# Two activation parts in one 512-column pass, with halves of a bank added on evacuation

## The chip, the cores and the metric

The kernel runs on one core of a Trainium2 chip. TensorE multiplies: it holds a block of 128 by 128 numbers (the stationary operand, brought by a weight load) and streams columns of the other operand past it, into PSUM. VectorE (DVE), ScalarE (ACT) and GpSimd (POOL) do the element-wise work, SyncE (SP) issues most of the transfers. The metric is the device time of one execution in microseconds (us); smaller is better.

## The reference, cut to what matters

Four residual layers over 256 tokens of 1024 features, and a final RMSNorm. Layers 0 and 3 mix tokens with Mamba-2, layer 1 with HGRN2, layer 2 with a gated DeltaNet (below: mamba, hgrn, gdn). Each layer then attends to 256 memory tokens and ends with a gated MLP that has a short convolution. Nearly all arithmetic is products of the 256 tokens with weight matrices, in float32:

```python
for i in range(DEPTH):                                   # DEPTH = 4
    x = x + mixer[i % 3](rmsnorm(x, ln_mix[i]), ...)     # in_w, then scan or recurrence, then out_w
    mem_n = rmsnorm(mem, ln_mem[i])
    x = x + memory_cross_attention(rmsnorm(x, ln_xattn[i]), mem_n, wq, wkv, wo)
    x = x + conv_glu_ffn(rmsnorm(x, ln_ffn[i]), up_w, conv_w, conv_b, down_w)

def conv_glu_ffn(h, up_w, conv_w, conv_b, down_w):       # d_ff = 2816
    gate, up = jnp.split(h @ up_w, 2, axis=-1)
    gate = causal_dwconv(gate, conv_w) + conv_b          # width 3
    return (jax.nn.silu(gate) * up) @ down_w
```

## The kernel before, in words

Features lie on the 128 partitions, tokens along the free dimension. Every product with a weight matrix is made of *steps*: one block of 128 by 128 weights times 256 tokens. To keep float32 accuracy each operand is split into a high and a low part of a format that TensorE takes in one pass (`wH`, `wL` for weights, `hH`, `hL` for activations), and `mm3` (line 164) adds up three products per step: high by high, low by high, high by low. Each of the three is a matmul of 256 columns with its own weight load.

Weights come in *pieces* of 128 by 1024 (8 steps). `prep` (line 150) issues a piece's transfer from SP into `raw`, rounds it to `wH` on ACT (line 158) and subtracts to get `wL` on DVE (line 159). There are 4 buffers of `raw` and 3 each of `wH` and `wL`; `prep` is moved some 300 instructions ahead of its place in the program, so weights are made while TensorE works on earlier ones.

`proj` (line 227) multiplies two pieces into the two halves of one PSUM bank of 512 columns. `ps_acc` (line 105) has four such banks, which rotate; the other four PSUM banks serve the mixers' short products. `out_proj` (line 252) keeps four banks open at once, one for each 256 output features. `mem_kv` (line 342) makes keys and values of the memory tokens; for the values the activations are the stationary operand and 256 weight columns stream.

What reads the bank: in the MLP `gate` (line 460) multiplies it by the token's norm on DVE (line 462) and convolves (lines 300 and 302); in mamba and gdn `conv` (line 295) reads the bank directly, once on ACT and three times on DVE; z is read by a Silu on ACT; keys are scaled on DVE (line 347).

The order of each engine's instructions is fixed when the program is built. A scheduler places instructions by a priority, program order with some groups moved ahead; TensorE's own order is that of the program, in which `Weave` (line 49) puts the mixers' short products among the long ones by a clock of charges (`tick(654)` for two steps). Each engine works its list strictly in order, so an instruction that waits holds up all behind it.

## Time and profile before

| | |
|---|---|
| median of 3 runs | 2111.76 us (2109.93 to 2115.88) |
| span of the profiled execution | 2112.4 us |
| TensorE busy | 2073.2 us, 98% |
| VectorE busy | 1590.7 us, 75% |
| ScalarE busy | 1282.7 us, 61% |
| GpSimd busy | 341.9 us, 16% |

The profiled execution's own time is its span, 2112.4 us, from the first to the last instruction; no time around it is listed apart, and it lies 0.6 us above the median of the runs. "Busy" is the time in which at least one instruction was under way; a matmul's row shows its whole way through the array, 0.28 us, though the next starts 0.12 us later, so rows of matmuls overlap and a busy TensorE is not one at its peak. What a stage can lose or win is read from stretches of the span, stage by stage.

### The profile page before, as it was taken

The numbers are of one execution on the slowest core, as the hardware profiler recorded it, in microseconds if no ns is written. First come the engines' busy times: TensorE is split into PE (matmuls) and PEld (weight loads), VectorE is DVE, ScalarE is ACT, GpSimd is POOL, SyncE is SP. The second block draws the span as 40 slices with busy tenths as digits, with TensorE's granted clock in tenths as the row PEclk, the third lists the DMA queues.
The fourth block names the chain that finished last, engine by engine and source line by source line (L and its number), as shares of the span: only waits on it lengthen the run. The fifth ranks groups of instructions, "written<-read, shape, count | busy, mean of one in ns | idle before, by whom it ended". The sixth has DMA issues, their size and how long they took to land.

```text
span 2112.4 us, 42162 instructions
## 1 busy us (share of the span) xinstructions
PE 2073.2 (98%) x17084; PEld 2022.5 (96%) x17084; DVE 1590.7 (75%) x2423; ACT 1282.7 (61%) x1874; POOL 341.9 (16%) x468
## 2 busy tenths in 40 slices
PE   8999999999999999999998999999999999999998
PEld 8999999999999899999998889999999999999997
DVE  6899787875689778866786775778756999777765
ACT  6677666554565566554676875666545777666553
POOL 2032211000133110001054450110001223101001
PEclk9999999999999999999999999999999999999999
DMA  6544545665644446655543333456555444545563
GB/s 237 165 152 151 157 146 163 204 189 170 195 159 138 141 132 197 193 185 183 183 127 124 112 127 102 136 164 202 188 170 186 156 150 151 163 138 176 185 188 111
DMA packets 110372, 343.10 MB, mean 162 GB/s; under 512 B 15456, under 2 KB 25312, under 8 KB 110176
## 3 DMA queue, kind: packets, MB, share of 16 engines
q1 hardware_dynamic: 106176, 333.42, 49.9%
q10 hardware_dynamic: 3744, 6.71, 1.0%
q8 instruction: 134, 2.20, 0.4%
q0 software_dynamic: 256, 0.26, 0.1%
q14 instruction: 62, 0.51, 0.1%
HBM read 336.42 MB, written 3.93 MB: 161 GB/s over the span
## 4 chain that ended last, share of the span: by engine, by line
PE 82%; issue 5%; DVE 5%; ACT 3%; POOL 2%; DMA 2%; SPq 0%; DVEq 0%; POOLq 0%; ACTq 0%
PE ffps L166 8%; PE ffps L168 8%; PE ffps L167 8%; PE acc L166 7%; PE acc L167 7%; PE acc L168 7%; PE mps L166 4%; PE mps L168 3%; PE mps L167 3%; PE kvps L167 2%; PE kvps L166 2%; PE kvps L168 2%; DVE wL L159 2%; PE qps L168 2%; PE qps L167 2%
## 5 line engine op out<-in xcount | busy, mean ns | idle before, releaser
L159 DVE TENSOR_TENSOR wL<-raw,wH 128x1024 fp32r<-128x1024 f32 (+2 forms) x639 | 775.2, 1214 | 348.5 <-ACT wH L158 347.0
L158 ACT CAST wH<-raw 128x1024 fp32r<-128x1024 f32 (+2 forms) x639 | 657.0, 1029 | 562.5 <-PE ffps L167 170.6
L166 PE MATMUL acc<-aH,wH 128*128 128x256 f32 x1408 | 402.3, 287 | 0.6 <-ACT aH L171 0.6
L168 PE MATMUL acc<-aH,wL 128*128 128x256 f32 x1408 | 399.2, 284 | 0.1
L167 PE MATMUL acc<-aL,wH 128*128 128x256 f32 x1408 | 398.6, 283 | 0.1
L166 PE MATMUL ffps<-hH,wH 128*128 128x256 f32 x1408 | 396.1, 282 | 1.8 <-ACT hH L181 1.8
L167 PE MATMUL ffps<-hL,wH 128*128 128x256 f32 x1408 | 396.0, 281 | 0.0
L168 PE MATMUL ffps<-hH,wL 128*128 128x256 f32 x1408 | 395.7, 281 | 0.0
L166 PEld LDWEIGHTS acc<-aH,wH 128*128 128x128 f32 x1408 | 269.1, 192 | 3.4 <-issue 1.3
L167 PEld LDWEIGHTS acc<-aL,wH 128*128 128x128 f32 x1408 | 269.9, 192 | 1.5 <-issue 0.5
L168 PEld LDWEIGHTS acc<-aH,wL 128*128 128x128 f32 x1408 | 269.9, 192 | 0.5 <-DVE wL L159 0.3
L166 PEld LDWEIGHTS ffps<-hH,wH 128*128 128x128 f32 x1408 | 265.0, 188 | 2.7 <-ACT hH L181 2.6
L168 PEld LDWEIGHTS ffps<-hH,wL 128*128 128x128 f32 x1408 | 265.3, 188 | 0.7 <-DVE wL L159 0.7
L167 PEld LDWEIGHTS ffps<-hL,wH 128*128 128x128 f32 x1408 | 265.3, 188 | 0.5
L166 PE MATMUL mps<-hH,wH 128*128 128x256 f32 x768 | 220.5, 287 | 0.0
L168 PE MATMUL mps<-hH,wL 128*128 128x256 f32 x768 | 215.9, 281 | 0.0
L167 PE MATMUL mps<-hL,wH 128*128 128x256 f32 x768 | 215.7, 281 | 0.0
L201 POOL TENSOR_TENSOR ns<-nsq 128x256 f32<-128x256 f32 x13 | 10.7, 827 | 880.4 <-ACT nsq L198 880.4
L166 PEld LDWEIGHTS mps<-hH,wH 128*128 128x128 f32 x768 | 144.7, 188 | 2.7 <-issue 2.4
L167 PEld LDWEIGHTS mps<-hL,wH 128*128 128x128 f32 x768 | 144.7, 188 | 0.3
L168 PEld LDWEIGHTS mps<-hH,wL 128*128 128x128 f32 x768 | 144.6, 188 | 0.1
L168 PE MATMUL gps<-hH,wL 128*128 128x256 f32 x448 | 128.0, 286 | 0.3 <-DVE wL L159 0.3
(397 smaller groups left out, 4514.5 us busy)
## 6 DMA issues: line engine op xcount, KB each, us to landing
raw<-f_up SPq DMA_DIRECT2D x176, 512.0 KB, 3.5
raw<-m_in SPq DMA_DIRECT2D x96, 512.0 KB, 3.5
raw<-f_down SPq DMA_DIRECT2D x80, 512.0 KB, 3.5
raw<-xa_kv SPq DMA_DIRECT2D x60, 512.0 KB, 3.8
raw<-g_in SPq DMA_DIRECT2D x48, 512.0 KB, 3.8
raw<-m_out SPq DMA_DIRECT2D x32, 512.0 KB, 3.5
raw<-xa_q SPq DMA_DIRECT2D x32, 512.0 KB, 3.6
raw<-xa_o SPq DMA_DIRECT2D x32, 512.0 KB, 3.5
```

The costliest lines, as they stand in the source:

```text
L158: ACT.copy(H[:, c], raw[:, c])
L159: DVE.tensor_tensor(out=L[:, c], in0=raw[:, c], in1=f32(H[:, c]), op=ALU.subtract)
L166: PE.matmul(dst, aH, bH, start=start, stop=False, skip_group_check=True)
L167: PE.matmul(dst, aH, bL, start=False, stop=False, skip_group_check=True)
L168: PE.matmul(dst, aL, bH, start=False, stop=stop, skip_group_check=True)
L201: self.eng.tensor_tensor(out=self.sum, in0=sq[:, :T], in1=sq[:, T:], op=ALU.add)
```

## The change

The high and low parts of the activations now lie side by side in one tile (`hh`), and one matmul of 512 columns passes both by the high weights (`mm2`); a second one of 256 columns adds high activations by low weights. A step has two matmuls instead of three. Its result fills a whole bank, whose two halves are added when it is read (`fold`: a copy of one half on ACT, an addition on DVE). So a product of two pieces takes two banks, and `ps_acc` has two buffers of two banks instead of four of one. `out_proj` of mixers and attention and hgrn's `proj_tok` keep `mm3`; the MLP's down product becomes `down_proj`, which makes the output in two halves. Values stream 512 weight columns, from two pieces made by `prep2` in a pool of their own. Convolutions and Silus read the folded copy in SBUF; the MLP's multiplication by the norm is on POOL for the first 20 of 22 tiles, and the split of its result is done as tiles come instead of in the down product. The charges of `tick` are adapted.

```diff
-    ps_acc = ctx.enter_context(tc.tile_pool(name="ps_acc", bufs=4, space=PSUM))
+    ps_acc = ctx.enter_context(tc.tile_pool(name="ps_acc", bufs=2, space=PSUM))
...
+    def banks(name):
+        return ps_acc.tile([P, 2, 512], F32, tag="acc", name=name)
     def bank(name):
-        return ps_acc.tile([P, 512], F32, tag="acc", name=name)
+        return banks(name)[:, 0, :]
...
-    hH = cst.tile([P, KT, T], F32R, name="hH")
-    hL = cst.tile([P, KT, T], F32R, name="hL")
+    hh = cst.tile([P, KT, 2, T], F32R, name="hh")
+    hH, hL = hh[:, :, 0, :], hh[:, :, 1, :]
...
+    def prep2(srcs, pool):
+        with tc.high_priority(offset=PRIO):
+            raw = pool.tile([P, 2, 1024], F32, tag="raw2", name="raw2")
+            H = pool.tile([P, 2, 1024], F32R, tag="wH2", name="wH2")
+            L = pool.tile([P, 2, 1024], F32R, tag="wL2", name="wL2")
+            for i in range(2):
+                nc.sync.dma_start(out=raw[:, i, :], in_=srcs[i])
+                ACT.copy(H[:, i, :], raw[:, i, :])
+                DVE.tensor_tensor(out=L[:, i, :], in0=raw[:, i, :], in1=f32(H[:, i, :]), op=ALU.subtract)
+        return H, L
...
+    def mm2(dst, wH, wL, both, start, stop):
+        PE.matmul(dst, wH, both, start=start, stop=False, skip_group_check=True)
+        PE.matmul(dst[:, :T], wL, both[:, 0, :], start=False, stop=stop, skip_group_check=True)
+    def fold(ps, dst, n=2):
+        ACT.copy(dst, ps[:, :n, T:])
+        return DVE.tensor_tensor(out=dst, in0=ps[:, :n, :T], in1=dst, op=ALU.add)
+    def proj(srcs, ps, both=None):
+        both = hh if both is None else both
         for i, s in enumerate(srcs):
             H, L = prep(s)
             for kt in range(KT):
                 c = slice(kt * P, (kt + 1) * P)
-                mm3(ps[:, i * T:(i + 1) * T], H[:, c], L[:, c], hH[:, kt, :], hL[:, kt, :],
-                    i == 0 and kt == 0, kt == KT - 1)
+                mm2(ps[:, i, :], H[:, c], L[:, c], both[:, kt], kt == 0, kt == KT - 1)
                 if kt % 2:
-                    weave.tick(654)
+                    weave.tick(616)
...
+    def down_proj(wsrc, nk, aa, last):
+        st = Stats(DVE if last else POOL)
+        ng = (nk + 3) // 4
+        for half in range(2):
+            accs = [banks(f"acc{j}") for j in range(2)]
+            for g in range(ng):
+                n = min(4, nk - 4 * g)
+                for j in range(2):
+                    H, L = prep(wsrc[g, 2 * half + j], n * T)
+                    for cb in range(2):
+                        for k in range(n):
+                            kt = 4 * g + k
+                            c = slice(k * T + cb * P, k * T + (cb + 1) * P)
+                            mm2(accs[j][:, cb, :], H[:, c], L[:, c], aa[:, kt], kt == 0, kt == nk - 1)
...
+        for b in range(4):
+            ps = banks("kvps")
...
+            fold(ps, KTt[:, 2 * b:2 * b + 2, :])
...
+        with phase(f"vw{layer}", 2) as vw:
+            for b in range(2):
+                ps = banks("vps")
+                for kh in range(2):
+                    H, L = prep2([io["xa_kv"][layer, 1, 2 * b + i, kh] for i in range(2)], vw)
+                    for mt in range(2):
+                        for k in range(4):
...
+                            mm3(ps[:, mt, :], mm[:, kt, 0, t], mm[:, kt, 1, t], H[:, :, c], L[:, :, c], kt == 0, kt == KT - 1)
...
-            def gate(t, ps):
-                gu = wk.tile([P, 2, T], F32, tag="gu", name="gu")
-                DVE.tensor_tensor(out=gu, in0=ps.rearrange("p (a b) -> p a b", a=2),
-                                  in1=rs.unsqueeze(1).to_broadcast([P, 2, T]), op=ALU.mult)
+            def gate(t, gu):
+                (DVE if t > 19 else POOL).tensor_tensor(out=gu, in0=gu, in1=rs.unsqueeze(1).to_broadcast([P, 2, T]), op=ALU.mult)
...
+                if t % 2:
+                    split(a2[-1], aa[:, t - 1:t + 1, 0, :], aa[:, t - 1:t + 1, 1, :])
...
+                ps = banks("ffps")
                 proj([io["f_up"][layer, 2 * t + i] for i in range(2)], ps)
-                todo.append((t, ps))
+                gu = wk.tile([P, 2, T], F32, tag="gu", name="gu", bufs=3)
+                fold(ps, gu)
+                todo.append((t, gu))
...
+                        src = np_.tile([P, 2, T], F32, tag="tmp", name="src", bufs=3)
+                        fold(ps, src)
                         for i in range(2):
                             ti = [16 + g, 24 + g, 2 * g, 2 * g + 1][2 * u + i]
-                            conv(cc[:, 2 * u + i, :], ps[:, i * T:(i + 1) * T], lambda j: pcol("m_cw", (ia * 32 + ti) * 4 + j),
+                            conv(cc[:, 2 * u + i, :], src[:, i, :], lambda j: pcol("m_cw", (ia * 32 + ti) * 4 + j),
```

Three places show what moves. The first is TensorE at the start of the first MLP's up product; `ffps` is the bank. Before:

```order
2544 L166 MATMUL ffps<-hH,wH 128x256
2545 L167 MATMUL ffps<-hL,wH 128x256
2546 L168 MATMUL ffps<-hH,wL 128x256
2547 L166 MATMUL ffps<-hH,wH 128x256
2548 L167 MATMUL ffps<-hL,wH 128x256
2549 L168 MATMUL ffps<-hH,wL 128x256
```

And of the change:

```order
1913 L245 MATMUL ffps<-hh,wH 128x512
1914 L246 MATMUL ffps<-hh,wL 128x256
1915 L245 MATMUL ffps<-hh,wH 128x512
1916 L246 MATMUL ffps<-hh,wL 128x256
1917 L245 MATMUL ffps<-hh,wH 128x512
1918 L246 MATMUL ffps<-hh,wL 128x256
```

The same 768 columns per step pass in two matmuls instead of three.

The second is VectorE while the keys of layer 2 are made. `KTt<-kvps` reads a bank of keys, `nh` and `hL` (after: `hh`) normalize the tokens for the mixer, and the `wL` of 384 columns is the first weight of the mixer. Before:

```order
955 L159 TENSOR_TENSOR wL<-raw,wH 128x1024
956 L171 TENSOR_TENSOR hL<-nh,hH 128x256 x2
957 L221 SCALAR_TENSOR_TENSOR nh<-xT,prm,nrs 128x256 x2
958 L347 TENSOR_TENSOR KTt<-kvps,rsm 128x512
959 L159 TENSOR_TENSOR wL<-raw,wH 128x1024
960 L171 TENSOR_TENSOR hL<-nh,hH 128x256 x2
961 L221 SCALAR_TENSOR_TENSOR nh<-xT,prm,nrs 128x256 x2
962 L159 TENSOR_TENSOR wL<-raw,wH 128x1024
963 L171 TENSOR_TENSOR hL<-nh,hH 128x256 x2
964 L347 TENSOR_TENSOR KTt<-kvps,rsm 128x512
965 L159 TENSOR_TENSOR wL<-raw,wH 128x1024 x6
966 L159 TENSOR_TENSOR wL<-raw,wH 128x384
```

And of the change, where row 997 folds the second bank pair of keys and row 999 the third:

```order
988 L163 TENSOR_TENSOR wL<-raw,wH 128x384
989 L237 SCALAR_TENSOR_TENSOR nh<-xT,prm,nrs 128x256
990 L187 TENSOR_TENSOR hh<-nh,hh 128x256
991 L237 SCALAR_TENSOR_TENSOR nh<-xT,prm,nrs 128x256
992 L187 TENSOR_TENSOR hh<-nh,hh 128x256
993 L237 SCALAR_TENSOR_TENSOR nh<-xT,prm,nrs 128x256
994 L187 TENSOR_TENSOR hh<-nh,hh 128x256
995 L237 SCALAR_TENSOR_TENSOR nh<-xT,prm,nrs 128x256
996 L187 TENSOR_TENSOR hh<-nh,hh 128x256
997 L251 TENSOR_TENSOR KTt<-kvps,KTt 128x512
998 L187 TENSOR_TENSOR hh<-nh,hh 128x256
999 L251 TENSOR_TENSOR KTt<-kvps,KTt 128x512
```

The reading of a bank of keys has moved behind the mixer's first weight and eight instructions of the normalization.

The third is VectorE in the first MLP, where the memory tokens of the next layer are split (`mL<-mtmp`, after: `mm<-mtmp`). Before:

```order
440 L462 TENSOR_TENSOR gu<-ffps,nrs 128x512
441 L159 TENSOR_TENSOR wL<-raw,wH 128x1024
442 L182 SCALAR_TENSOR_TENSOR mL<-mtmp,prm,mH 128x256 x3
443 L159 TENSOR_TENSOR wL<-raw,wH 128x1024
444 L182 SCALAR_TENSOR_TENSOR mL<-mtmp,prm,mH 128x256 x3
445 L462 TENSOR_TENSOR gu<-ffps,nrs 128x512
446 L159 TENSOR_TENSOR wL<-raw,wH 128x1024
```

And of the change:

```order
440 L163 TENSOR_TENSOR wL<-raw,wH 128x1024
441 L529 TENSOR_TENSOR a_4153<-c,gu 128x256
442 L163 TENSOR_TENSOR wL<-raw,wH 128x1024
443 L198 SCALAR_TENSOR_TENSOR mm<-mtmp,prm,mm 128x256 x3
444 L163 TENSOR_TENSOR wL<-raw,wH 128x1024
445 L198 SCALAR_TENSOR_TENSOR mm<-mtmp,prm,mm 128x256 x3
446 L251 TENSOR_TENSOR gu<-ffps,gu 128x512 x2
```

Two folds now stand together behind two weight pieces and six splits of memory tokens.

## Rows read from the trace of the kernel before

**Rows 1.** Page, part 1: busy us, share, instructions of each engine.
```profile
PE 2073.2 (98%) x17084; PEld 2022.5 (96%) x17084; DVE 1590.7 (75%) x2423; ACT 1282.7 (61%) x1874; POOL 341.9 (16%) x468
```

**Rows 2.** Waits of TensorE: total us, times, longest; the two longest rows.
```profile
PE kvps L166 <- ACT wH L158: 6.6, 1, 6.6
PE grp L1033 <- ACT S L1028: 4.8, 2, 3.0
```

**Rows 3.** Stretches: mamba (layer 0), MLP up, MLP down, hgrn, gdn.
```profile
core 0: us, PE busy (x) PEld busy (x) DVE busy (x) ACT busy (x) POOL busy (x), PEclk, DMA share, GB/s
60.00:226.00 166.00, 165.33 (x1362) 157.60 (x1360) 154.39 (x272) 120.99 (x170) 40.11 (x34) 1.00 0.48 153
...
338.00:464.00 126.00, 125.56 (x1055) 125.03 (x1055) 100.49 (x145) 72.35 (x104) 3.35 (x5) 1.00 0.61 192
464.00:527.00 63.00, 63.00 (x528) 63.00 (x527) 33.79 (x37) 30.14 (x36) 1.18 (x2) 1.00 0.56 171
...
574.00:686.00 112.00, 111.96 (x946) 105.34 (x945) 98.80 (x148) 65.92 (x90) 36.22 (x18) 1.00 0.47 150
...
1021.00:1250.00 229.00, 217.70 (x1739) 205.23 (x1738) 181.21 (x358) 173.64 (x259) 96.08 (x218) 0.99 0.41 131
```

**Rows 4.** TensorE in order of time, split products: start us, duration us.
```profile
1000.07 0.28 PE L166 MATMUL kvps<-wH,mH 128*128 128x256 f32 x1
1000.19 0.28 PE L167 MATMUL kvps<-wL,mH 128*128 128x256 f32 x1
```

**Rows 5.** TensorE in order of time, plain float32 products of gdn.
```profile
1070.28 1.03 PE L911 MATMUL gp<-kq 128*128 128x256 f32 x4
1071.14 0.27 PE L949 MATMUL gkp<-ident,kq 128*128 128x128 f32 x1
```

**Rows 6.** Groups by line and shape, MLP up: xcount, busy us, mean ns, idle before.
```profile
L166 PE MATMUL ffps<-hH,wH 128*128 128x256 f32 x1408 | 396.1, 282 | 1.8 <-ACT hH L181 1.8
```

**Rows 7.** Groups by line and shape, VectorE, ScalarE and GpSimd.
```profile
L159 DVE TENSOR_TENSOR wL<-raw,wH 128x1024 fp32r<-128x1024 f32 x612 | 757.5, 1239 | 323.9 <-ACT wH L158 322.5
L158 ACT CAST wH<-raw 128x1024 fp32r<-128x1024 f32 x612 | 641.3, 1048 | 528.9 <-PE ffps L167 170.6 <-PE acc L167 140.6 <-PE kvps L168 42.0
...
L204 POOL TENSOR_TENSOR ns<-ns,nsq 128x256 f32<-128x256 f32 x78 | 76.7, 983 | 47.4 <-ACT nsq L198 43.2
...
L462 DVE TENSOR_TENSOR gu<-ffps,nrs 128x512 f32<-128x512 f32 x88 | 60.3, 689 | 19.3 <-PE ffps L168 18.9
...
L302 DVE SCALAR_TENSOR_TENSOR cc<-mps,prm,cc 128x255 f32<-128x255 f32 x64 | 30.5, 476 | 0.1
...
L171 ACT CAST pH<-pt 128x512 fp32r<-128x512 f32 x16 | 9.4, 590 | 4.7 <-PE pt L418 4.7
```

**Rows 8.** VectorE in order of time, in mamba of layer 0.
```profile
123.32 1.21 DVE L159 TENSOR_TENSOR wL<-raw,wH 128x1024 fp32r<-128x1024 f32 x1
124.45 0.48 DVE L554 TENSOR_SCALAR E<-rb,tcol 128x256 f32<-128x256 f32 x1
...
125.49 0.68 DVE L171 TENSOR_TENSOR aL<-yT,aH 128x512 fp32r<-128x512 f32 x1
126.09 0.68 DVE L594 TENSOR_TENSOR yT<-yT,sz 128x512 f32<-128x512 f32 x1
```

**Rows 9.** A line of VectorE: duration ns min/median/max, first and last start.
```profile
L182 DVE SCALAR_TENSOR_TENSOR hL<-xT,prm,hH x64: 471/478/972, 270.4 to 1914.1; 128x256 fp32r<-128x256 f32 x64
```

**Rows 10.** A line of VectorE in mamba, the same columns.
```profile
L605 DVE SCALAR_TENSOR_TENSOR yT<-yT,prm,rs x32: 471/798/1243, 114.4 to 1835.3; 128x256 f32<-128x256 f32 x32
```

**Rows 11.** Groups by line and shape, VectorE in the normalization.
```profile
L221 DVE SCALAR_TENSOR_TENSOR nh<-xT,prm,nrs 128x256 f32<-128x256 f32 x32 | 14.1, 479 | 0.6 <-ACT nrs L213 0.5
...
L171 DVE TENSOR_TENSOR hL<-nh,hH 128x256 fp32r<-128x256 f32 x32 | 12.4, 420 | 0.6 <-ACT hH L171 0.2
```

**Rows 12.** Stretches of 3 us at the start of the queries of layer 1.
```profile
721.00:724.00 3.00, 2.13 (x13) 1.53 (x13) 3.00 (x5) 1.43 (x3) 1.31 (x3) 0.97 0.27 109
724.00:727.00 3.00, 3.00 (x16) 3.00 (x16) 0.93 (x2) 1.04 (x1) 1.41 (x2) 0.50 0.58 175
```

More of the change, by code (lines that the diff above doesn't have):

```diff
@@ L250, in proj_tok, with new_x, add, out_proj @@
                         weave.tick(654)
-    def out_proj(wsrc, nk, a, gens=None, gname=None, layer=0, last=False):
-        accs = [bank(f"acc{b}") for b in range(4)]
-        ng = (nk + 3) // 4
-        st = Stats(DVE if last else POOL)
+    def new_x(b, add, st, gname, layer, last):
+        xs = flat(xT[:, 2 * b:2 * b + 2, :])
+        add(xs)
+        if gname is not None:
+            for kt in (2 * b, 2 * b + 1):
+                split_gain(xT[:, kt, :], pcol(gname, layer * 8 + kt), hH[:, kt, :], hL[:, kt, :])
+        st.add(xs)
+        if last:
+            for kt in (2 * b, 2 * b + 1):
+                fg = pcol("final", kt)
+                if b < 3:
+                    POOL.tensor_scalar(out=KTt[:, kt, :], in0=xT[:, kt, :], scalar1=fg, scalar2=None, op0=ALU.mult)
+                else:
+                    ACT.activation(out=KTt[:, kt, :], in_=xT[:, kt, :], func=AF.Copy, scale=fg)
+    def down_proj(wsrc, nk, aa, last):
+        st = Stats(DVE if last else POOL)
+        ng = (nk + 3) // 4
+        for half in range(2):
[9 more added lines that the diff above has]
+                            mm2(accs[j][:, cb, :], H[:, c], L[:, c], aa[:, kt], kt == 0, kt == nk - 1)
+                    if g == ng - 1:
+                        def add(xs, ps=accs[j]):
+                            x3 = xs.rearrange("p (a b) -> p a b", a=2)
+                            for i in range(2):
+                                DVE.tensor_tensor(out=x3, in0=x3, in1=ps[:, :, i * T:(i + 1) * T], op=ALU.add)
+                        new_x(2 * half + j, add, st, None, 0, last)
+        return st
+    def out_proj(wsrc, nk, a, gens=None, gname=None, layer=0):
+        accs = [banks(f"acc{b}") for b in range(2)]
+        accs = [accs[b // 2][:, b % 2, :] for b in range(4)]
+        ng = (nk + 3) // 4
+        st = Stats()
         for g in range(ng):
@@ L384, in attention @@
+                            weave.tick(600)
+                for mt in range(2):
+                    ACT.activation(out=Vt[:, mt, b * 512:(b + 1) * 512], in_=ps[:, mt, :], func=AF.Copy, scale=rsmc[:, mt:mt + 1])
     def attention(layer, st):
@@ L743, in hgrn @@
             for pr in range(4):
-                ps = bank("fps")
+                ps = banks("fps")
                 proj([io["h_in"][ib, pr, i] for i in range(2)], ps)
                 e1 = W("e1", 1)
-                ACT.activation(out=flat(e1), in_=ps, func=AF.Exp, scale=-1.0)
+                fold(ps, e1)
+                ACT.activation(out=e1, in_=e1, func=AF.Exp, scale=-1.0)
                 DVE.tensor_scalar(out=e1, in0=e1, scalar1=1.0, scalar2=None, op0=ALU.add)
@@ L1065, in unit @@
             def unit(piece, tis, cc):
-                ps = bank("gps")
+                ps = banks("gps")
                 proj([io["g_in"][ic, piece + i] for i in range(2)], ps)
-                if tis is not None:
-                    with tc.high_priority(offset=EVAC):
-                        for i in range(2):
-                            conv(cc[:, i, :], ps[:, i * T:(i + 1) * T], lambda j: pcol("g_cw", tis[i] * 4 + j), 4, None)
-                return ps
+                with tc.high_priority(offset=EVAC):
+                    if tis is None:
+                        fold(ps, cc)
+                        return
+                    src = np_.tile([P, 2, T], F32, tag="tmp", name="src", bufs=3)
+                    fold(ps, src)
+                    for i in range(2):
+                        conv(cc[:, i, :], src[:, i, :], lambda j: pcol("g_cw", tis[i] * 4 + j), 4, None)
             gens = []
```

121 lines of the change are left out of this document (50 added, 71 removed).

## The prediction

> **What bounds the kernel now.** I read the page's busy times first: TensorE 2073.2 us of a span of 2112.4 [rows 1]. Overlapping rows make a matmul engine look busy, so I next read who TensorE waited for: the longest entries are 6.6 us, once, at the start, and 4.8 us in two waits [rows 2]. It waits for almost nothing, so TensorE's own list sets the time. Third, the stretches by stage: the reader should compare VectorE with the length of each. It is busy 154.39 of 166 us in mamba, 98.80 of 112 in hgrn, 100.49 of 126 in the MLP's up product, 181.21 of 229 in gdn [rows 3]. So TensorE is the bound everywhere, and in mamba VectorE stands 11.6 us behind it. Last, TensorE in order of time: split matmuls of 256 columns start 0.12 us apart [rows 4]. The clock is granted in full there, the 2.4 GHz level, at which 256 columns would take 106.7 ns. Some 13.3 ns of each interval are not columns.
>
> **What those 13.3 ns are.** In plain float32 the same shape starts 0.86 / 4 = 215 ns apart [rows 5], two clock periods for each of 256 columns (213.3 ns) and only 2 ns more, though each of these matmuls too has its own load of 128 by 128 weights. [...] Where 512 split columns stream, their 213.3 ns hide the next load as rows 5 do: I take 216 ns. The 256 columns that follow hide the next load no better than now: 120 ns. The bounds for 512 columns are 213 (columns alone) and 240 (twice rows 4).
>
> **What is removed.** A step falls from 3 x 120 = 360 to 216 + 120 = 336 ns. Steps that change: MLP up 1408 [rows 6], mamba 768, gdn 384, queries 256, hgrn 192, MLP down 704, keys 256; 3968 in all, counted from the loops (pieces times 8). 3968 x 24 ns = 95.2 us. Values: 256 steps of 3 x 120 ns become 128 of 3 x 216 ns, 92.2 against 82.9, 9.2 us less. Together **104.4 us**, to 2008.0, if nothing else becomes late.
>
> **What is added to ScalarE and VectorE.** A fold is a copy of 512 columns out of PSUM, 590 ns on ScalarE, and an addition of 512 on VectorE, for which the MLP's multiplication is the nearest row, 689 ns [rows 7]; back to back such an operation holds VectorE 0.60 us, a weight piece 1.13 [rows 8]. Products with a fold: 48 in the mambas, 88 in MLPs, 24 in gdn, 16 queries, 12 in hgrn, 16 keys. Keys and the MLP had one reading of that size already.
>
> *Mamba.* VectorE needs 154.4 + 24 x 0.60 = 168.8 us, TensorE now 166 - 384 x 0.024 = 156.8. VectorE becomes the bound: 12 us given back in each of two layers, **24**. Some of its list can slip into the output product behind, and some will wait; I let these cancel. Bounds: 0 and 40.
>
> *MLP up.* 100.5 + 22 x 0.60 for folds + 11 x 0.60 for splits that were in the down product - 20 x 0.60 for multiplications now on POOL = 108.3 us, against 126 - 8.4 = 117.6 on TensorE. This hides, but the POOL work costs VectorE something: a line with two SBUF inputs that reads 478 ns as its median reaches 972 [rows 9], and in mamba another has a median of 798 where its least is 471 [rows 10]; there POOL is busy 40.11 us of 166 [rows 3]. With 0.5 us for each of 20 multiplications VectorE comes to 118.3, just late: 2 us a layer, **8** (0 to 40).
>
> *Keys.* With two buffers, the fourth product of the keys needs the bank pair of the second. Its fold stands in VectorE's list behind the mixer's first weight piece, and that piece's buffer is free only when TensorE is through with the third product (the change's second place in the order). From there: rounding (0.5 to 1.05 us), subtraction (0.5 to 1.13), then normalization at 0.40 and 0.34 us each (durations 479 and 420 less the overlap) [rows 11], then the fold. Layer 1: 1.05 + 1.13 + 3 x 0.40 + 5 x 0.34 + 0.60 = 5.7; layer 2, whose first piece is small (0.5 us each, by proportion), 0.5 + 0.5 + 4 x 0.74 + 0.60 = 4.6; layer 3 about 4.6. In layer 0 the first fold stands behind two weight pieces of that kind, about 5. TensorE stands still: **20**. With four banks it had two products more to go on with.
>
> *Where the memory tokens are split.* In three MLPs two folds stand behind a weight piece that waits for the product before (the third place). ScalarE: 1.05 + 3 x 0.40 + 0.50 for the copy, then 0.60 and some 0.2 of signals: 3.6 us each, **11**. At the start of each mamba the softplus chain and a weight piece stand so before a fold, 1.05 + 1.13 + 0.60 + 0.3 = 3.1 us, **6**.
>
> *gdn.* The tile for z is now claimed before the head two places back has freed it, so its fold waits for that head's end and one of two bank pairs is held meanwhile; the next products run in a single pair and wait for their folds, 1.4 us plus the queue. About four such places at 2 us: **8** (0 to 20). hgrn, 98.8 + 12 x 0.60 = 106 us of VectorE against 107.4, and the two halves of the down product, whose first bank pair must be read before the second half starts: **6** together (2 to 12).
>
> *The clock.* After 3 us in which TensorE was busy 2.13, the granted clock reads 0.50, the 1.2 GHz level, and TensorE shows 16 matmuls in 3 us [rows 12] where 25 fit at 0.12: 1.1 us lost. Eight of the new standstills last 3 us or more: **9**.
>
> The sum: 2112.4 - 104.4 + 24 + 8 + 20 + 11 + 6 + 8 + 6 + 9 = 2100.0. The span is 0.6 us over the median, which I leave. **2100 us**, 0.6% faster. A measurement tells no change from one within 0.3% here, 2105.4 to 2118.1.
>
> **The rivals.**
>
> *The buffers absorb it (faster).* VectorE's backlog in mamba slips into the output product, and gdn's other products cover its folds. For it: TensorE shows 98% although VectorE is at 93% in mamba. Against it: 168.8 is over 156.8 whatever the order. Left are the standstills that the order fixes, 20 + 11 + 6 and 4 for the clock: 2008 + 41 = 2049.
>
> *VectorE loses to POOL (slower).* Every convolution in mamba, which now has two SBUF inputs where the bank was one at 476 ns [rows 7], and every convolution and weight piece of the MLP meets POOL as in rows 9 and 10. A POOL addition of 256 takes 983 ns, so a multiplication of 512 is about 1.7, 34 us in each MLP. It decides once VectorE is past TensorE's 117.6, that is from 0.47 us for each multiplication; at 0.75 it adds 20 x 0.25 x 4 = 20 us, and mamba's convolutions about 4 each: 2128. Against it: weight pieces have a mean of 1239 over all stages, near the 1.21 of one alone [rows 7, 8].
> The Trainium skill ("SBUF — State Buffer", section Who interferes with whom) states that a VectorE instruction with two SBUF inputs and a GpSimd instruction that reads SBUF shut each other out for the whole instruction. By that rule the 34 us would come on top of 108.3 in each MLP, 25 us over TensorE, and the time would be near 2190; the mean of 1239 for weight pieces speaks against so much, and I give it 2 in 100.
>
> *The excess goes with each matmul (slower).* If 512 columns start 226.7 ns apart, a step is 346.7 ns and the saving 3968 x 13.3 ns + 5.1 = 58 us. The losses to VectorE shrink to 76, as TensorE is later: 2130. Against it: rows 5. At 240 ns nothing is saved, 2177.
> The Trainium skill ("TensorE: Matmul & The Clock Gate", section Back-to-back issue gap) gives columns over 2.4 GHz plus 2.5 ns, 109 and 216 ns; the trace's 0.12 us disagrees at 256. By it a step would have been 327.5 and become 325, and the time would be near 2165; 1 in 100.
>
> **How the numbers follow.** My forecast 45 in 100, with 2080 to 2120 as its own range; absorbed 23; VectorE and POOL 18 with the 2 of the rule; the excess 13 with its 1; the rest spread. Faster: three fifths of the forecast (27) and the absorbed (23), 50. Within 0.3%: a quarter of the forecast and a few of each slower rival, 19. Slower: 31. The range leaves out one in ten on either side: 2055, under which only a wholly absorbed case lies, and 2140, above which the rules and the upper bounds lie.
>
> **What would show it.** Starts of `ffps` matmuls 0.216 and 0.120 us apart (0.227 or 0.240: the excess rival). Mamba's stretch as long as now or longer, with VectorE at 95% or more; if it is under 160 us, absorbed is right. In the keys one idle time of TensorE of about 5 us a layer, released by a fold; in three MLPs one of 3 to 4. MLP up near 122 us; 130 or more is POOL's doing. I am wrong altogether if TensorE shows waits under 40 us in sum and the time is still over 2100, or if the down products, where VectorE is busy 33.79 of 63 us [rows 3], do not shorten by about 3 us each.

## The result and the profile after

| | before | after |
|---|---|---|
| median of 4 runs | 2111.73 us (2109.93 to 2115.88) | 2344.23 us (2338.53 to 2347.89) |
| ratio, 95% interval | | 1.109 [1.107, 1.112] |
| span of the profiled run | 2112.4 us | 2336.7 us |

The change made the kernel 11% slower, far outside the range of the prediction. What answers to [rows 1] in the page after:

```profile
PE 2129.8 (91%) x12732; PEld 1835.8 (79%) x12732; DVE 1729.3 (74%) x2551; ACT 1385.6 (59%) x2066; POOL 490.1 (21%) x564
```

TensorE went from 98% to 91%. Its waits (answer to [rows 2]; total us, times, longest) name the reason in the first lines: it waits for folds (L251), for the additions that read down's bank pairs (L314), and in the mambas for a sum on GpSimd (`s`, L664), which is no reader of a product. All its waits add up to 195 us, before to 31 us.

```profile
PE ffps L245 <- DVE gu L251: 30.6, 8, 10.2
PE kvps L245 <- DVE KTt L251: 22.8, 4, 6.9
PE gn L667 <- POOL s L664: 19.2, 10, 4.2
PE acc L245 <- DVE xT L314: 12.2, 4, 3.1
PE gps L245 <- DVE src L251: 11.4, 3, 4.6
PE kvps L245 <- DVE xT L314: 9.1, 3, 3.1
```

The stretches, in the order of [rows 3] (mamba of layer 0, MLP up, MLP down, hgrn, gdn):

```profile
66.00:248.00 182.00, 169.31 (x987) 140.80 (x986) 175.96 (x285) 128.54 (x190) 42.03 (x34) 0.98 0.43 136
368.00:513.00 145.00, 131.40 (x728) 112.18 (x729) 116.47 (x151) 88.08 (x134) 36.72 (x26) 0.96 0.54 167
513.00:583.00 70.00, 65.29 (x355) 56.07 (x354) 35.73 (x42) 30.39 (x35) 2.21 (x3) 0.95 0.53 165
640.00:752.00 112.00, 111.65 (x753) 95.96 (x752) 100.59 (x155) 72.06 (x101) 36.87 (x18) 1.00 0.45 139
1125.00:1388.00 263.00, 230.05 (x1333) 192.87 (x1332) 192.16 (x369) 186.70 (x278) 89.23 (x206) 0.92 0.36 112
```

Mamba is 16 us longer, up 19, down 7, gdn 34; hgrn is the same, though its folds and products changed too. The granted clock (the column behind the engines', 1.00 is the 2.4 GHz level) fell in every stretch that grew.

The second thing to see is the spacing of the products (answer to [rows 4]; TensorE in order of time, start and duration): the up projection, the values, and the up projection behind a stop.

```profile
417.97 0.40 PE L245 MATMUL ffps<-hh,wH 128*128 128x512 f32 x1
418.21 0.28 PE L246 MATMUL ffps<-hh,wL 128*128 128x256 f32 x1
418.33 0.39 PE L245 MATMUL ffps<-hh,wH 128*128 128x512 f32 x1
...
439.39 0.63 PE L245 MATMUL ffps<-hh,wH 128*128 128x512 f32 x1
439.82 0.41 PE L246 MATMUL ffps<-hh,wL 128*128 128x256 f32 x1
440.03 0.63 PE L245 MATMUL ffps<-hh,wH 128*128 128x512 f32 x1
...
1794.76 0.39 PE L182 MATMUL vps<-wH,mm 128*128 128x512 f32 x1
1794.99 0.39 PE L183 MATMUL vps<-wL,mm 128*128 128x512 f32 x1
```

512 columns take 0.24 us, not 0.216 (over all up products at the full clock the median is 232 ns, a quarter at 229 or less, a quarter at 240 or more; the values' 227), and 256 take 0.12. Behind the stop, at the 1.2 GHz level, the same two take 0.43 and 0.21.

A reckoning from the starts of TensorE's list: intervals over 0.7 us add up to 214.6 us (98 of them), before 24.8 us (18), so 190 us more. Products that start while the clock is at its half fill 114.9 us, before 13.4; half of that is extra, 51 us more. 190 + 51 = 241, which is 17 more than the growth of the span, 224.3. In those 17 must lie what the wide products gain; they were not taken apart further.

One of the stops, at the memory tokens of layer 0 (ScalarE, VectorE and TensorE, a fence each, in order of time, with the idle time before and its releaser):

```profile
427.10 1.05 ACT L162 CAST wH<-raw 128x1024 fp32r<-128x1024 f32 x1 [0.51 <-issue]
431.99 0.51 ACT L197 ACTIVATE mm<-mtmp,prm 128x256 fp32r<-128x256 f32 x1 [3.84 <-DMA mtmp<-mem]
...
435.74 0.89 ACT L197 ACTIVATE mm<-mtmp,prm 128x256 fp32r<-128x256 f32 x2
436.54 0.56 ACT L250 COPY gu<-ffps 128x512 f32<-128x512 f32 x1
```

```profile
435.87 1.28 DVE L198 SCALAR_TENSOR_TENSOR mm<-mtmp,prm,mm 128x256 fp32r<-128x256 f32 x3
437.14 1.29 DVE L251 TENSOR_TENSOR gu<-ffps,gu 128x512 f32<-128x512 f32 x2
```

```profile
437.98 0.76 PE L245 MATMUL ffps<-hh,wH 128*128 128x512 f32 x1 [9.91 <-DVE gu L251]
```

The fold's copy (L250) stands on ScalarE behind the tokens' split (L197), which waits 3.84 us for its DMA; the two folds on VectorE come behind it, and TensorE stands still for 9.9 us. The same stop comes in the MLPs of layers 1 and 2 (9.4 and 10.2 us), and TensorE's clock is at its half for 10.2 us at each. Before, ScalarE waited for this DMA as well, and TensorE ran on:

```profile
388.49 0.91 ACT L181 ACTIVATE mH<-mtmp,prm 128x256 fp32r<-128x256 f32 x2 [2.63 <-DMA mtmp<-mem]
```

### The profile page after: what moved, and what is told of

Read it like the earlier page. It is cut to its first block, busy times and chain, and to the rows that moved or that the text cites. A ratio compares the mean times of both kernels' runs of the same rounds, so it can differ in the third digit from the quotient of the medians.

```text
span 2336.7 us, 33880 instructions
## 1 busy us (share of the span) xinstructions
PE 2129.8 (91%) x12732; PEld 1835.8 (79%) x12732; DVE 1729.3 (74%) x2551; ACT 1385.6 (59%) x2066; POOL 490.1 (21%) x564
## 5 line engine op out<-in xcount | busy, mean ns | idle before, releaser
L163 DVE TENSOR_TENSOR wL<-raw,wH 128x1024 fp32r<-128x1024 f32 (+1 forms) x611 | 757.1, 1241 | 315.0 <-ACT wH L162 313.2
L162 ACT CAST wH<-raw 128x1024 fp32r<-128x1024 f32 (+1 forms) x611 | 622.6, 1020 | 429.0 <-PE acc L245 125.2
L245 PE MATMUL ffps<-hh,wH 128*128 128x512 f32 x1408 | 510.2, 404 | 40.0 <-DVE gu L251 30.6
L246 PE MATMUL ffps<-hh,wL 128*128 128x256 f32 x1408 | 399.1, 283 | 6.1 <-DVE wL L163 6.1
L245 PEld LDWEIGHTS ffps<-hh,wH 128*128 128x128 f32 x1408 | 267.2, 190 | 115.1 <-issue 30.3
L245 PE MATMUL mps<-hh,wH 128*128 128x512 f32 x768 | 284.2, 409 | 4.1 <-DVE src L251 4.1
L246 PEld LDWEIGHTS ffps<-hh,wL 128*128 128x128 f32 x1408 | 268.5, 191 | 9.5 <-DVE wL L163 8.6
L245 PE MATMUL acc<-aa,wH 128*128 128x512 f32 x704 | 253.2, 402 | 14.3 <-DVE xT L314 12.2
L246 PE MATMUL mps<-hh,wL 128*128 128x256 f32 x768 | 218.0, 284 | 0.0
L523 POOL TENSOR_TENSOR gu<-gu,nrs 128x512 f32<-128x512 f32 x80 | 133.2, 1669 | 380.8 <-DVE gu L251 325.8
L246 PE MATMUL acc<-aa,wL 128*128 128x256 f32 x704 | 198.9, 283 | 4.4 <-DVE wL L163 4.4
L245 PE MATMUL gps<-hh,wH 128*128 128x512 f32 x448 | 171.6, 419 | 15.3 <-DVE src L251 11.4
L245 PEld LDWEIGHTS acc<-aa,wH 128*128 128x128 f32 x704 | 134.8, 191 | 48.8 <-issue 13.4
```

The source lines that it names most:

```text
L162: ACT.copy(H[:, c], raw[:, c])
L163: DVE.tensor_tensor(out=L[:, c], in0=raw[:, c], in1=f32(H[:, c]), op=ALU.subtract)
L245: PE.matmul(dst, wH, both, start=start, stop=False, skip_group_check=True)
L246: PE.matmul(dst[:, :T], wL, both[:, 0, :], start=False, stop=stop, skip_group_check=True)
L523: (DVE if t > 19 else POOL).tensor_tensor(out=gu, in0=gu, in1=rs.unsqueeze(1).to_broadcast([P, 2, T]), op=ALU.mult)
```

## The experiments

Theory A: TensorE waits because only two products can be under way, so that every delay of a reader becomes a stop, and the clock falls behind the stops. Theory B: the folds' load on VectorE, ScalarE and GpSimd is the cause. Beside both: the wide pass saves less than was forecast. Ratios are to the kernel before, with 95% intervals; the two kernels with one weight piece leave out the other up weights, were run once each (2283.55 us of the changed kernel, 2111.4 of before) and stand in no row.

| kernel | median us | ratio |
|---|---|---|
| before, two pairs | 2222.49 | 1.053 [1.051, 1.055] |
| before, with the folds' load | 2180.38 | 1.033 [1.031, 1.034] |
| before, wide values | 2120.77 | 1.004 [1.003, 1.006] |
| before, wide up products, eight banks | 2107.91 | 0.9983 [0.9971, 0.9995] |
| before, wide up and down products, eight banks | 2104.59 | 0.9961 [0.9948, 0.9975] |
| after, products of 256 | 2357.09 | 1.116 [1.113, 1.119] |
| after, folds first | 2333.55 | 1.106 [1.104, 1.108] |
| after, down as it was | 2319.30 | 1.098 [1.096, 1.100] |
| after, gate on VectorE | 2307.71 | 1.093 [1.091, 1.094] |
| after, gate on VectorE, up four deep | 2289.38 | 1.084 [1.082, 1.086] |

### The kernel before with two pairs

```diff
-    ps_acc = ctx.enter_context(tc.tile_pool(name="ps_acc", bufs=4, space=PSUM))
+    ps_acc = ctx.enter_context(tc.tile_pool(name="ps_acc", bufs=2, space=PSUM))
...
+    def banks(name):
+        return ps_acc.tile([P, 2, 512], F32, tag="acc", name=name)
     def bank(name):
-        return ps_acc.tile([P, 512], F32, tag="acc", name=name)
+        return banks(name)[:, 0, :]
...
-        accs = [bank(f"acc{b}") for b in range(4)]
+        accs = [banks(f"acc{b}") for b in range(2)]
+        accs = [accs[b // 2][:, b % 2, :] for b in range(4)]
```

> The kernel before, its three products of 256 columns and its evacuations unchanged, but its products rotate over two pairs of banks (only one bank of a pair used) as in the changed kernel, where before they rotate over four banks. Theory A (TensorE waits because a pair has to be read out within the time of one other pair, and its reader stands in a queue behind other work): much of the loss is there without any change of arithmetic, 2180 to 2280 us, with the 10 us stop at the memory-token place of the MLPs and some 6 us at the keys of each later layer. Theory B (the loss is the work of the folds, and what it does to VectorE and GpSimd): within 15 us of 2112.

110 us: A's number. Only the buffers were edited, but the scheduler makes the lists of the engines anew for them, TensorE's too, which is not that of the program alone. In both mambas TensorE comes to the first transposes (`tp`) after 96 matmuls of the mamba's products in place of 137, as it does in the changed kernel, and waits 5.3 us there for VectorE:

```profile
PE tp L542 <- DVE pk L533: 10.5, 2, 5.3
```

So the 110 us are the price of two pairs together with the order made for them; what the waiting costs alone was not separated.

Not A's places: at the memory tokens and the keys it lost little (one wait of 3.3 us on the keys' evacuation). Over half of the loss sits in the mixers (33 us in gdn, 13 in each mamba), 10 us come before the first mamba, and from a mixer's output product to the end of up each layer takes 6 to 11 us more. The stretches of gdn and of most of an up projection:

```profile
1066.00:1328.00 262.00, 232.61 (x1750) 218.80 (x1749) 188.06 (x363) 175.07 (x260) 92.20 (x223) 0.93 0.37 117
366.90:497.00 130.10, 126.61 (x1048) 125.51 (x1047) 100.39 (x143) 72.61 (x104) 1.89 (x3) 0.99 0.59 186
```

gdn takes the 262 us of the changed kernel; an up projection is 8 to 10 us longer from its start to its end, of which 3 are 24 matmuls of the attention's output that now stand among its first ones. The largest wait of TensorE in gdn, and the mean clock of the run:

```profile
PE gps L170 <- DVE gc L307: 12.8, 5, 5.4
```

```profile
core 0: 2221.8 us, clock 0.982
```

The wait is for the convolution (L307) that reads a product out of its bank; the kernel before, with two more products to go on with, shows no such wait in gdn. (1 - 0.982) / 0.5 of 2221.8 us are 80 us at the half clock; before, at a mean of 0.995, it was 21.

### The kernel before with the folds' load

```diff
+    def load(ps):
+        junk = np_.tile([P, 512], F32, tag="nsq", name="junk", bufs=2)
+        ACT.copy(junk, ps)
+        DVE.tensor_tensor(out=junk, in0=ps, in1=junk, op=ALU.add)
                 proj([io["f_up"][layer, 2 * t + i] for i in range(2)], ps)
+                load(ps)
...
```

> The kernel before with four rotating banks and its own products and evacuations, and beside them, for each unit of keys, queries, up projections and mixer projections, one ScalarE copy and one VectorE addition of 512 columns from the unit's bank, whose result nobody reads: the work of the folds without their place in the chain. With the two shown runs (before 2112, two pairs without folds 2222, two pairs with folds 2357) it fills a square of depth and folds. If the folds cost what they weigh on the engines: 2112 + 135 = 2245 us. If they cost because a pair is held through them while there are only two: at most 2135, with the rise in the two mamba stages, where VectorE has 154 us of work in 167.

Neither number: 69 us, between 23 and 135. In the stretches (mamba, its output product, up) the loss is in mamba and behind it:

```profile
61.00:245.00 184.00, 172.26 (x1337) 159.88 (x1336) 154.55 (x273) 130.39 (x186) 35.42 (x29) 1.00 0.44 138
245.00:306.00 61.00, 56.75 (x438) 52.56 (x437) 48.17 (x70) 36.01 (x54) 15.10 (x14) 1.00 0.45 137
368.00:494.00 126.00, 125.55 (x1056) 125.02 (x1055) 109.56 (x163) 83.13 (x125) 3.65 (x5) 1.00 0.62 193
```

The longest waits of TensorE over the whole run begin with this row, and the mean clock is:

```profile
PE yp L598 <- POOL E L590: 18.5, 30, 1.7
```

```profile
core 0: 2178.8 us, clock 0.995
```

Mamba with its output product takes 29 us more, twice, and gdn's output product some 10. Up is where it was, to 0.1 us, with VectorE at 109.56 of 126. VectorE is at 84% in mamba, so it is not full there; TensorE waits for E, a result of a chain over three engines, of which the folds are put ahead. Whether the load or the new order delays it was not separated. The clock did not fall: 51 intervals over 0.7 us here, 56 in the run with two pairs, but the longest 3.2 us here and 5.7 us there. Four deep, the load made many short stops; two deep, without the load, there were long ones.

### The changed kernel with products of 256

```diff
-        PE.matmul(dst, wH, both, start=start, stop=False, skip_group_check=True)
+        PE.matmul(dst[:, :T], wH, both[:, 0, :], start=start, stop=False, skip_group_check=True)
+        PE.matmul(dst[:, T:], wH, both[:, 1, :], start=False, stop=False, skip_group_check=True)
```

> The changed kernel with the 512-column product replaced by two of 256 into the same two halves of the bank; folds, buffers and order otherwise alike. By the term of the prediction (24 ns a step, 3968 steps) the time rises by 95 us to 2440. By what the changed kernel's trace shows (a step of 349 to 360 ns against 358) it rises by 0 to 40 us, 2345 to 2385. Below 2335 would say that the wide pass costs something of its own.

13 us more. The wide pass is worth some 13 us over 3968 steps in this surrounding, not 95. It is a rough number: the four runs of the two kernels spread over 13 and 9 us.

### One weight piece for a whole up projection, after and before

```diff
+            H, L = prep(io["f_up"][layer, 0])
             for t in range(NFF):
                 ps = banks("ffps")
-                proj([io["f_up"][layer, 2 * t + i] for i in range(2)], ps)
+                for i in range(2):
+                    for kt in range(KT):
+                        c = slice(kt * P, (kt + 1) * P)
+                        mm2(ps[:, i, :], H[:, c], L[:, c], hh[:, kt], kt == 0, kt == KT - 1)
...
```

> The changed kernel with one weight piece for a whole up projection (the layer's other up weights are left out), so that no piece is loaded or split while it runs. If the step is bound by the products themselves: 349 ns in the mean and 123 us of products, and stops only at the memory tokens (about 10 us). If the 512-column product is slowed by the pieces' traffic: below 340 ns. If the folds wait because of the pieces in their queues, the waits for gu go from the first units too.

> The kernel before with one weight piece for a whole up projection (the others are left out): the price of a step of three 256-column products without the pieces' traffic. By the trace of before 358 ns and 126 us a layer; if that traffic is part of the price, less, and the difference to the changed kernel's step under the same condition is what the wide pass is worth: 24 ns by the prediction, under 10 by the comparison that kept the folds.

The up projection of layer 1 in the changed kernel (without its first and last products):

```profile
841.00:963.00 122.00, 119.47 (x687) 103.95 (x686) 55.85 (x104) 45.37 (x86) 29.70 (x25) 1.00 0.07 22
```

and that of layer 0 in the kernel before:

```profile
338.00:464.00 126.00, 125.43 (x1056) 124.98 (x1055) 53.06 (x102) 31.59 (x61) 3.38 (x5) 1.00 0.06 18
```

With DMA at 0.06 and VectorE at half its work, a step of before stays at 357.8 ns (119.25 between starts), and one of the changed kernel has a mean of 354 to 359 in the four layers (intervals under 0.5 us). So the pieces' traffic is no part of a step's price. The pieces are part of the stops, by their place in the queues or by their work, which this does not separate: the changed up projection takes 130 to 132 us here, where it took 138 to 147, its stop at the memory tokens shrinks to 1.6 to 2.2 us (I had left it 10), and its clock is full.

### The kernel before with wide values

```diff
-                ps = bank("kvps")
+                ps = [bank("vps") for mt in range(2)]
...
-                                mm3(d, mH[:, kt, t], mL[:, kt, t], H[:, c], L[:, c], first, last)
+                            mm3(ps[mt], mH[:, kt, t], mL[:, kt, t], H[:, :, c], L[:, :, c], kt == 0, kt == KT - 1)
```

> The kernel before with only the values' products changed to 512 weight columns. 384 products at 227 ns in place of 768 at 120 ns: 5 us faster, 2107. If the pairs of pieces, which come two at a time, hold TensorE up at the start of each 512-column stretch: 2112 or more.

8 us slower. All of it is in layer 0, where mamba's first product starts at 65.5 us in place of 57.1; keys and values of layer 1 take what they took, 46.6 us against 46.5. What the values gain there (21.8 us in place of 23.0), the keys give back (24.9 in place of 23.5).

### The changed kernel with the folds first

```diff
     def fold(ps, dst, n=2):
-        ACT.copy(dst, ps[:, :n, T:])
-        return DVE.tensor_tensor(out=dst, in0=ps[:, :n, :T], in1=dst, op=ALU.add)
+        with tc.high_priority(offset=2 * PRIO):
+            ACT.copy(dst, ps[:, :n, T:])
+            return DVE.tensor_tensor(out=dst, in0=ps[:, :n, :T], in1=dst, op=ALU.add)
```

> The changed kernel with every fold put ahead of waiting weight pieces and of the memory tokens' and the norm's work in the order of ScalarE and VectorE. Theory A: the 10 us stops at the memory-token places (30 us in all) and those of the keys (23 us) shrink, and with them the half-clock stretches; 2240 to 2300. Theory B (load): the same work is only in another order, 2330 or more.

11 us: B's number, and a miss for A as I had put it. The stops it aimed at did shrink: up 134 to 138 us in place of 138 to 147, gdn 250 in place of 263, no stop over 4 us in the keys of the later layers. But mamba takes 192 us in place of 182, hgrn 121 in place of 112 and gdn's output product 94 in place of 88. The longest wait of TensorE is now one for a fold, that of z in the mambas:

```profile
PE mps L245 <- DVE sz L252: 30.2, 10, 3.6
```

Its copy now comes in ScalarE's list before its destination is free: ScalarE waits 11.4 us, in four, for the last reader of an earlier `sz` on VectorE. A fold put first can come too early for its own buffer. In gdn's output product TensorE waits for weight pieces (3.5 us, where it waited 0.6).

### The changed kernel with down as it was, and with the gate on VectorE

```diff
-                            mm2(accs[j][:, cb, :], H[:, c], L[:, c], aa[:, kt], kt == 0, kt == nk - 1)
+                        mm3(accs[b][:, cb * T:(cb + 1) * T], H[:, c], L[:, c], aa[:, kt, 0, :], aa[:, kt, 1, :],
+                            kt == 0 and cb == 0, kt == nk - 1)
...
-                (DVE if t > 19 else POOL).tensor_tensor(out=gu, in0=gu, in1=rs.unsqueeze(1).to_broadcast([P, 2, T]), op=ALU.mult)
+                DVE.tensor_tensor(out=gu, in0=gu, in1=rs.unsqueeze(1).to_broadcast([P, 2, T]), op=ALU.mult)
```

> The changed kernel with the down projections as they were: three products of 256 columns, four blocks accumulated at once in the four banks, one addition to x a block (the parts of the MLP's activations still come from the new layout). The prediction priced the two halves of down with hgrn's at 6 us in all; the trace shows 66.7 to 69.5 us a layer against 63.2, with a 3.3 us gap at the switch of the halves. If the halves and their bank pairs are what costs: 63 to 64 us a layer, 2315 to 2325. If down is slowed by what comes before it (the clock, the pieces): no more than 5 us gained, 2340.

> The changed kernel with every gate product of the MLP on VectorE instead of GpSimd for 20 of 22 units. VectorE gets 14 us more a layer, the pieces' differences are no longer drawn out while GpSimd runs (1241 ns in the mean, up to 1970). If GpSimd is a cause of the 138 to 147 us: 130 to 138 us and 2300 to 2330. If depth is: unchanged or up to 10 us slower.

Down as it was: 25 us less, as expected of the halves. Its stretch in layer 0:

```profile
513.00:577.00 64.00, 63.27 (x522) 62.60 (x521) 34.04 (x39) 29.15 (x34) 0.74 (x1) 1.00 0.59 177
```

The gate on VectorE: 37 us less, up 135 to 141 us a layer, which is 28 of the 37. Groups of the changed kernel (xcount, busy us, mean ns, idle before):

```profile
L245 PE MATMUL ffps<-hh,wH 128*128 128x512 f32 x1408 | 510.2, 404 | 40.0 <-DVE gu L251 30.6 <-DVE hh L198 6.0 <-ACT wH L162 1.4
L523 POOL TENSOR_TENSOR gu<-gu,nrs 128x512 f32<-128x512 f32 x80 | 133.2, 1669 | 380.8 <-DVE gu L251 325.8 <-ACT nrs L229 40.8 <-PE ffps L245 14.2
```

The same groups with the gate on VectorE:

```profile
L245 PE MATMUL ffps<-hh,wH 128*128 128x512 f32 x1408 | 503.3, 400 | 19.4 <-DVE gu L251 12.2 <-DVE hh L198 6.0 <-ACT wH L162 1.3
L523 DVE TENSOR_TENSOR gu<-gu,nrs 128x512 f32<-128x512 f32 x88 | 60.0, 686 | 0.7
```

VectorE does 80 products more and TensorE waits 18 us less for its folds. But those waits were nearly all at the memory tokens, and there ScalarE's list has changed with the gate: a fold's copy now stands among the splits and not behind them all, and the stop is 2.0 to 3.4 us in place of 9.4 to 10.2. ScalarE with the gate on VectorE:

```profile
433.63 0.57 ACT L250 COPY gu<-ffps 128x512 f32<-128x512 f32 x1
...
435.04 0.91 ACT L197 ACTIVATE mm<-mtmp,prm 128x256 fp32r<-128x256 f32 x2
```

In layer 3, whose MLP has no memory tokens to split, the up projection gains 3 us of the 28. What GpSimd itself costs shows in two ways. A gate takes 1669 ns in place of 686, and ScalarE waits for it 101 us in all. And it holds up VectorE: splits of the MLP's activations (duration min, median, max), with the gate on GpSimd and on VectorE:

```profile
L187 DVE TENSOR_TENSOR aa<-a,aa x44: 684/1784/1847, 398.9 to 2267.0; 128x512 fp32r<-128x512 f32 x44
L187 DVE TENSOR_TENSOR aa<-a,aa x44: 680/686/697, 398.0 to 2235.9; 128x512 fp32r<-128x512 f32 x44
```

The weight pieces of the up projections have a mean of 1304 ns with the gate on GpSimd and of 1223 without. The Trainium skill ("SBUF — State Buffer", section Who interferes with whom) has a VectorE instruction with two SBUF inputs and a GpSimd instruction that reads SBUF shut each other out. The trace agrees: these splits and pieces have two SBUF inputs, a gate of 1272 ns at its shortest reaches 2334, and the fold's addition, which has one input in PSUM, keeps its 680 to 692 ns. The prediction had priced the gate at 1.7 us and taken it for hidden. How the 37 us divide between GpSimd and the new order at the tokens was not separated.

### Four products under way again

The changed kernel with the gate on VectorE, every second up unit in two of the mixers' banks:

```diff
+                if t % 2 == 0:
+                    ps = banks("ffps")
...
+                else:
+                    pss = [mx("ffps") for i in range(2)]
+                    for i in range(2):
+                        proj([io["f_up"][layer, 2 * t + i]], pss[i].unsqueeze(1))
+                        fold(pss[i].unsqueeze(1), gu[:, i:i + 1, :], 1)
```

> The changed kernel with the gate product on VectorE (2308 us as it stands) and every second up unit in two of the mixers' banks, so that four units are under way in place of two; nothing else differs. Theory A (depth): the up stretch falls from 136 to 141 us to 126 to 129, half-clock stretches in it go, and the kernel takes 2255 to 2275 us. Theory B (the folds' load on VectorE, 121 of 126 us): 133 us or more a layer, 2300 or more.

The kernel before with the wide pass and folds in the up products alone, and the mixers' banks in turn:

```diff
-                ps = bank("ffps")
-                proj([io["f_up"][layer, 2 * t + i] for i in range(2)], ps)
+                pss = [(mx if t % 2 else bank)("ffps") for i in range(2)]
...
+                        PE.matmul(pss[i], H[:, c], hh[:, kt], start=kt == 0, stop=False, skip_group_check=True)
+                        PE.matmul(pss[i][:, :T], L[:, c], hH[:, kt, :], start=False, stop=kt == KT - 1, skip_group_check=True)
...
+                    ACT.copy(gu[:, i, :], pss[i][:, T:])
+                    DVE.tensor_tensor(out=gu[:, i, :], in0=pss[i][:, :T], in1=gu[:, i, :], op=ALU.add)
```

> The kernel before with the 512-column pass and folds in the up projections of the MLPs alone, a unit in two single banks, and the units taken in turn from the products' four banks and the mixers' four, which stand idle there: four units deep as before. Theory A (depth): the up stretch takes 352 steps of 350 to 360 ns, 123 to 127 us in place of 126.4, and the kernel 2095 to 2115. Theory B (load: VectorE gets some 0.95 us a unit more, 121 of 126 us): 135 us or more a layer, 2150 or more.

The changed kernel's first units of up and the rest of it, and in the fence behind, an up projection of the kernel before with wide products:

```profile
367.00:375.00 8.00, 5.93 (x38) 4.76 (x37) 5.43 (x8) 4.32 (x9) 3.22 (x4) 1.00 0.45 154
375.00:500.00 125.00, 123.69 (x696) 106.65 (x696) 111.08 (x176) 85.30 (x140) 1.57 (x2) 1.00 0.60 190
```

```profile
1393.00:1519.00 126.00, 125.27 (x710) 108.51 (x709) 111.52 (x186) 84.14 (x147) 4.03 (x5) 1.00 0.60 193
```

In both, TensorE runs through the stretch at the full clock with VectorE at 111 us: in the up projection depth decides, not load. In the changed kernel up is 132.6 to 133.0 us in place of 135.2 to 140.9, above the 126 to 129 that I expected and just under B's 133: some 3 us are matmuls of the attention's output among its first products, and 3 are waits of these for tokens and weight pieces. That gives 18 us, and I had forecast 33 to 53: 2289 misses the range, though not by load. In the kernel before, 88 wide units with their folds cost nothing; the step there is 355.2 to 356.9 ns against 357.8. The 4 us by which its median is lower do not lie in up: in the profiled runs the four up projections take 507.6 us against 506.8, and gdn with its output product 304.7 against 308.6, where before has two stretches at the half clock and this run none. Runs of the kernel before alone go from 2107 to 2117 us, with mean clocks from 0.998 to 0.994, so that the wide pass gains anything in up is not shown.

### A faster version

The same kernel with the down products of three layers wide as well, all four blocks at once in eight banks.

```diff
+        accs = [[(bank if b < 2 else mx)(f"acc{b}") for cb in range(2)] for b in range(4)]
...
+                        PE.matmul(accs[b][cb], H[:, c], both[k], start=kt == 0, stop=False, skip_group_check=True)
+                        PE.matmul(accs[b][cb][:, :T], L[:, c], both[k][:, 0, :], start=False, stop=kt == nk - 1,
+                                  skip_group_check=True)
```

> An attempt at a faster kernel: the kernel before with the 512-column pass in the up projections, units in turn from the products' and the mixers' banks (2107.9 us), and also in the down projections of three layers, all four blocks at once in eight banks. A down step took 350.6 us a thousand in the changed kernel against 360: 176 steps, 1.6 us a layer, 5 us in three layers: 2100 to 2106. If the four additions a block in place of one, or the mixers' banks held to the end of down, delay the next layer's keys: 2108 or more.

2104.6 us, 0.4% faster than the kernel before and the fastest of all. In the profiled runs 4.6 us of it lie in the three wide down projections, as expected; most of the rest is again in gdn (305.1 us against 308.6). So the wide pass pays in down where it keeps its depth, and in up it costs nothing. Down, layer 1:

```profile
907.00:968.00 61.00, 61.00 (x353) 53.78 (x352) 36.01 (x45) 30.22 (x37) 0.56 (x1) 1.00 0.53 176
```

(In that expectation "350.6 us a thousand" is 350.6 ns a step.)

## Why the prediction was wrong

It forecast 104 us of savings and 92 of losses; the runs show a saving of some 13 and losses of some 245.

- **The step's price.** "I take 216 ns" failed, and with it 82 of the 95.2 us. No run shows 216 for split operands, and none less than 223: 512 columns take 227 to 240 ns, 256 take 117 to 121. The excess over columns at 2.4 GHz (213.3 and 106.7) is 14 to 27 and 10 to 14 ns, so it grows with the columns; the prediction had it hidden behind longer ones. [Rows 5] were of plain float32 and did not carry over to split operands. The rival "the excess goes with each matmul" had the direction and 226.7, but kept 58 us. What the step saves depends on its place: 1 to 3 ns in up, 9 in down (350.6 against 360).
- **The values**, 9.2 us: they gain nothing after layer 0, and lose 8 us there.
- **The depth.** The prediction saw that two pairs follow four banks and priced single standstills that the order showed: keys 20, memory tokens 11, mamba's start 6, gdn 8. The keys were right (22.8 us of waits, at most 6.9), and so was mamba's start (1.5 and 2.1 us in each of two). The other two failed: two pairs and the order made for them cost 110 us with no fold in the program, 33 of it in gdn and 13 in each mamba. "About four such places at 2 us" treated as a list of stops what is a loss of slack for every product whose reader comes late. At the memory tokens a split was priced by its instructions (3.6 us), not by the DMA that it waits for (3.84 of the 9.9 us): 29.5 us of waits in three, where 11 were forecast. With a fold's copy among the splits each was 2.0 to 3.4 us.
- **GpSimd**, 8 us: moving the gate is worth 37, most of it by way of the memory tokens' stop. The prediction's own figures (118.3 against 117.6) give 0.7 us a layer, not the 2 that it took, and the 0.5 us of VectorE for each gate was right: over 80 gates the 44 splits and the weight pieces of up lose some 42 us, in four MLPs, and not the 34 us in each of the rival's rule. Its sign "130 or more is POOL's doing" did not hold: with the gate on VectorE up is still 135 to 141 us. **The halves of down**, within 6 us: 25, since the second half waits for the reading of the first (3.1 us) and so do the next layer's keys (3.1 us). By the prediction's own sign, that down does not shorten, it was wrong altogether: down is 7 us longer, and where depth is kept some 1.5 shorter.
- **Mamba**, 24 us: 30 in the stretches and 10 in the output products. The test named (as long as now or longer, VectorE at 95% or more) came out: 175.96 of 182. But the load alone, with depth, cost 58 there at 84%, so a full VectorE is not the whole of it.
- **The clock**, 9 us: 51, which are contained in the losses above. It was priced by eight long stops; there are 29 stretches at the half clock, before 5. The Trainium skill ("TensorE: Matmul & The Clock Gate", section A second HAM failure mode: psum-queue depth-cycling) tells of a kernel that cycles through its PSUM banks, idles briefly between groups, and loses throughput to a clock that goes down and up. The trace agrees: two pairs in place of four banks took the mean clock from 0.995 to 0.982.

A check on the whole: 110 (depth) + 69 (load) + 37 (gate) + 25 (halves) + 8 (values) - 13 (wide pass) = 236, against 232 measured. The parts come from two different kernels, and the keys' stops stand in neither of the first two terms (they need folds and shallow depth together), so the agreement is a check on sizes, not a proof that they add.

Open stay why the price goes with the columns for split operands, how much of the price of two pairs is waiting and how much the order made for them, how much of mamba's loss is load and how much order, and how much of the gate's is GpSimd.

## What to carry to other kernels

Where a product takes twice the PSUM, price the lost depth before the saved cycles: run the old kernel with the new number of buffers, a change of a few lines, which here told half of the loss. An edit of buffers or engines also makes the lists of all engines anew: compare the order before a difference is put down to the edit. A spacing in the trace is a price only for its own operand type: measure the wide product before multiplying by thousands. A read-out step added to a chain is free while other products are ready to run, as in up four deep (111 us of VectorE work in 126), and each of its delays is a stop when none are.

## What was not expected of the hardware

Split products of 256 and 512 columns run at nearly one price per column, 0.46 and 0.45 ns, where plain float32 products of 256 take 0.84 for two clock periods each. The granted clock fell with long stops of TensorE and not with many short ones: 51 intervals over 0.7 us of at most 3.2 us left it at 0.995 (the folds' load), 56 of up to 5.7 us took it to 0.982 (two pairs); the changed kernel has 98 of up to 10.5 us and 0.965. A GpSimd instruction of 1.3 us can hold up VectorE for its length: a split with two SBUF inputs took 1784 ns in the median with the gate on GpSimd, 686 without.
